# Row maxima taken with the additions in two dilated groups, and chunk-end keys made from chunk-middle keys, in a hybrid decoder layer

## The chip, the cores and the metric

The kernel runs on one core of a Trainium2 chip. The metric is the device time of one execution in microseconds, as the median of several runs. Five engines work side by side, each through its own queue in order: PE (TensorE, matrix products), DVE (VectorE), ACT (ScalarE), POOL (GpSimd) and SP (SyncE, which here only issues transfers). They wait for each other through semaphores.

## The reference, cut to what matters

One decoder layer on 512 tokens of 1024 features: a SwiGLU half-step, a token-mixing step, a second SwiGLU half-step. The token mixing has three branches; the change touches two of them.

The first is a gated linear recurrence in chunks of 64 tokens (4 heads, 128 key and 128 value dimensions):

```python
b = jnp.cumsum(jnp.log(f), axis=2)
ref = b[:, :, C // 2 - 1:C // 2]
scores = jnp.einsum('bnchk,bnshk->bnhcs', q * jnp.exp(b - ref), k * jnp.exp(ref - b))
...
b_last = b[:, :, -1:]
kv = jnp.einsum('bnshk,bnshv->nbhkv', k * jnp.exp(b_last - b), v)
```

The second is attention in three dilated groups (4 heads each): group 0 in blocks of 128 neighbours, group 1 with every fourth token, group 2 with every sixteenth. Each group adds an ALiBi bias and a mask to its scores, takes the row maximum, exponentials and their sum; the groups are then weighted against each other by maxima and sums:

```python
s = s - slopes[:, None, None] * (delta * dil).astype(jnp.float32)
s = jnp.where(valid[:, None], s, -jnp.inf)
m = jnp.max(s, axis=-1)
p = jnp.exp(s - m[..., None])
```

The third branch, attention of the tokens into 256 memory tokens, is not edited, but its work stands next to the edited work in the queues.

## The kernel before, in words

Weights and activations are split into a high part and a rest, and each product is made of three matmuls (lines 381 and 399 to 401). Pairs of weight columns are projected together in seven block products (`pair`, line 411); their operands are sums of weight quarters, made on DVE (tiles `sum`, `sh`, `st`) and split by ACT (line 173) and DVE (line 168) into tiles `w`. Line 168 is the helper `tt`, through which nearly every DVE addition, subtraction or multiplication of two tensors goes, so DVE rows are told apart by their tiles. The copy of line 438 takes the first of a pair's four results out of its PSUM bank (pool `ps`, 5 banks).

`mixing` (line 1107) runs the steps of `ORDER`: the two recurrence pairs (`hg0`, `hg1`), the preparation of the memory (`prep`, whose norm is in `normed`, lines 198 to 211: squares on ACT in line 186, a factor on DVE in line 192 and POOL in line 195, the scaling on DVE in line 204, transposes on PE in line 390), the dilated pairs (`dil0`, `dil1`, two heads each), the queries for the memory (`mq0`, `mq1`) and the three output branches. Elementwise work of a step is a generator that is continued when the projected PE time has advanced by the latencies in `LAT`; a scheduler then places the instructions of each engine in an order from its own estimates, so an edit in one place can move rows of its neighbours.

In `hgrn` (line 801), for each of two heads: `b` is the running sum of the logarithms; line 836 subtracts the chunk's middle, line 837 subtracts `b` from the chunk's last value, over 128x512; five exponentials follow on ACT (lines 841 to 845; line 843 is that of the chunk-end difference, line 845 makes the 128x8 decays); four multiplications on DVE make `qd`, `kd`, `kl` and `qe`. `hgrn_out` (line 858) multiplies `kd` by `qd` on PE, transposes `kl`, forms the states and the output. Its two small tiles `hss` and `hr` have four buffers.

In `dil_scores` (line 914), group 0 adds the bias and takes the maximum in one DVE instruction (line 928; in the trace CUSTOM_DVE_ANT_0, with a DVE_READ_ACCUMULATOR2_ANT that writes the maximum). Groups 1 and 2 put the scores of four 128x128 blocks into one PSUM bank (pool `px`, 3 banks, shared by all the elementwise steps), add the bias in two DVE additions of 128x256 (line 936), and for group 2 take the maxima of groups 1 and 2 together by two reductions over 128x512 (line 938). Line 943 scales the maximum into `nm`, and four exponentials with sums follow on ACT (line 946).

`mem_attention` (line 763) makes scores on PE (line 386), maxima on DVE (lines 774 and 775), exponentials on ACT (line 778, which also frees the `px` bank), and after a division (lines 779 and 782) transposes, copies (line 790) and a product with the values.

Of the kernel before, what the change touches and what calls it, by code (L numbers as in the profile page):

```python
# [8 lines left out]
F32 = mybir.dt.float32  # L9
F32R = mybir.dt.float32r  # L10
U32 = mybir.dt.uint32
AF = mybir.ActivationFunctionType
ALU = mybir.AluOpType
AX = mybir.AxisListType
# [3 lines left out]
P = 128  # L18
T = 512
NT = T // P  # L20
# [10 lines left out]
NCH = T // CHUNK  # L31
# [21 lines left out]
class Layer:  # L53
# [747 lines left out]
    def hgrn(self, hp, f, q, og, vh, out):  # L801

        nc = self.nc
        heads = [2 * hp, 2 * hp + 1]
        ch = lambda x: x.rearrange("p (n c) -> p n c", c=CHUNK)
        full = [P, NCH, CHUNK]
        step = LAT['hg']

        qs = [self.slot() for _ in heads]
        for i in range(2):  # L810
            nc.scalar.activation(f[i], f[i], AF.Sigmoid)
            nc.scalar.activation(qs[i], q[i], AF.Sigmoid)
        for i in range(2):
            nc.scalar.activation(og[i], og[i], AF.Sigmoid)
        k = []
        for i, hd in enumerate(heads):
            lb, omlb = self.lb[:, hd:hd + 1], self.omlb[:, hd:hd + 1]
            yield step
            nc.vector.tensor_scalar(out=f[i], in0=f[i], scalar1=omlb, scalar2=lb, op0=ALU.mult, op1=ALU.add)
            k.append(self.slot())  # L820
            nc.vector.tensor_scalar(out=k[i], in0=f[i], scalar1=-1.0, scalar2=1.0, op0=ALU.mult, op1=ALU.add)
            self.tt(q[i], q[i], qs[i], ALU.mult)
        for i in range(2):
            nc.scalar.activation(f[i], f[i], AF.Ln)
        b, kd, qd, qe, kl, dec = [], [], [], [], [], []
        for i in range(2):
            yield step
            b.append(self.slot())
            nc.vector.tensor_tensor_scan(out=b[i], data0=self.reset, data1=f[i], initial=0.0, op0=ALU.mult, op1=ALU.add)
        for i in range(2):  # L830
            yield step
            ref = ch(b[i])[:, :, CHUNK // 2 - 1:CHUNK // 2]
            last = ch(b[i])[:, :, CHUNK - 1:CHUNK]
            kd.append(self.slot())
            kl.append(self.slot())
            self.tt(ch(kd[i]), ch(b[i]), ref.broadcast_to(full), ALU.subtract)
            self.tt(ch(kl[i]), last.broadcast_to(full), ch(b[i]), ALU.subtract)
            qd.append(self.slot())
            qe.append(self.slot())
            dec.append(self.sm(NCH, "dec"))  # L840
            nc.scalar.activation(qd[i], kd[i], AF.Exp)
            nc.scalar.activation(kd[i], kd[i], AF.Exp, scale=-1.0)
            nc.scalar.activation(kl[i], kl[i], AF.Exp)
            nc.scalar.activation(qe[i], b[i], AF.Exp)
            nc.scalar.activation(dec[i], last.rearrange("p n o -> p (n o)"), AF.Exp)
        for i in range(2):
            yield step
            self.tt(qd[i], qd[i], q[i], ALU.mult)
            self.tt(kd[i], kd[i], k[i], ALU.mult)
            yield step  # L850
            self.tt(kl[i], kl[i], k[i], ALU.mult)
            self.tt(qe[i], qe[i], q[i], ALU.mult)
        yield LAT['hgx']
        for i, hd in enumerate(heads):
            yield from self.hgrn_out(hd, kd[i], qd[i], kl[i], qe[i], dec[i], og[i], vh)
            out[hd] = og[i]

    def hgrn_out(self, hd, kd, qd, kl, qe, dec, og, vh):
        nc = self.nc
# [17 lines left out]
        st = [self.slot((P, 4, P)) for _ in range(2)]  # L877
# [20 lines left out]
            self.mm(po[rs, n // 2, :], qe[:, n * CHUNK:(n + 1) * CHUNK], state[n - 1], False, True, skip_group_check=True)  # L898
        sq = self.slot((P, NT, P))
        nc.scalar.activation(sq, po, AF.Square)  # L900
        ss, r = self.sm(NT, "hss"), self.sm(NT, "hr")
        nc.vector.tensor_reduce(out=ss, in_=sq, axis=AX.X, op=ALU.add)
        nc.vector.tensor_scalar(out=ss, in0=ss, scalar1=1.0 / P, scalar2=EPS, op0=ALU.mult, op1=ALU.add)
        nc.gpsimd.tensor_tensor(out=r, in0=ss, in1=self.mhalf, op=ALU.pow)
# [9 lines left out]
    def dil_scores(self, nb, g, q, k, s, st, then=None):  # L914

        nc = self.nc
        yield LAT['dil0']  # L920
        if g == 0:
            for j in range(NT):
                lo = max(0, j - 1) * P
                n = (j + 1) * P - lo
                sp = self.paux((P, n))
                self.mm(sp, q[:, j * P:(j + 1) * P], k[:, lo:lo + n])
                out = s[j // 2][:, j % 2, :, :].rearrange("p a b -> p (a b)")[:, 2 * P - n:]
                nc.vector.tensor_tensor_reduce(out=out, in0=sp, in1=nb[:, 2 * P - n:2 * P], scale=1.0, scalar=-3.0e38,
                                               op0=ALU.add, op1=ALU.max, accum_out=st[:, j, 0:1])
        else:  # L930
            sp = self.paux((P, 4, P))
            for a in range(4):
                self.mm(sp[:, a, :], q[:, a, :], k[:, a, :])
            nb = nb[:, (g + 1) * P:(g + 2) * P].unsqueeze(1).broadcast_to([P, 2, P])
            for i in range(2):
                self.tt(s[i][:, :, g - 1, :], sp[:, 2 * i:2 * i + 2, :], nb, ALU.add)
                if g == 2:
                    nc.vector.tensor_reduce(out=st[:, 2 * i:2 * i + 2, 0:1], in_=s[i].rearrange("p a g b -> p a (g b)"), axis=AX.X, op=ALU.max)  # L938
        if then is None:
            return  # L940
        yield LAT['exp']
        nm = self.sm(4, "nm")
        nc.vector.tensor_scalar(out=nm, in0=st[:, :, 0], scalar1=-SCALE, scalar2=None, op0=ALU.mult)
        for i in range(4):
            b = self.dil_block(s, i, g == 0)
            nc.scalar.activation(b, b, AF.Exp, bias=nm[:, i:i + 1], scale=SCALE, accum_out=st[:, i, 1:2])
            if i == 1:
                yield LAT['exp']
        then()
# [393 lines left out]
```

## Time and profile before

| what | value |
|---|---|
| median of 3 runs | 1344.18 us (1342.6 to 1344.91) |
| profiled execution, its own time | 1344.03 us |
| its span, first to last instruction | 1342.3 us |
| mean granted TensorE clock in it | 0.998 |
| DVE busy | 1042.6 us (78%) in 1976 instructions |
| ACT busy | 755.4 us (56%) in 1557 instructions |
| POOL busy | 88.4 us (7%) |

The page gives busy time of each engine, the chain of work that ended last, and groups of instructions with the idle time before them and what ended it. The trace behind it gives every instruction with its start and length. An instruction's length is longer than its share of the engine, because the next one starts before it ends; the distance from start to start is the share. Matmul ends are modelled, so waits of PE are read from starts. The edited work lies between 425 and 760 us.

### The profile page before, as it was taken

What the parts mean: (1) busy time and instruction counts of PE and PEld (TensorE: products, weight loads), DVE (VectorE), ACT (ScalarE), POOL (GpSimd) and SP (SyncE); (2) the same over time, 40 slices, a digit from 0 to 9 for tenths busy, and PEclk for the clock granted to TensorE, in tenths of its full rate; (3) what the DMA queues carried; (4) which work ended last, traced back from release to release, by engine and by line L of the source; (5) the groups of instructions that cost most, each with busy time, mean ns of one, the idle gap of its engine ahead of it and who ended that gap; (6) DMA issues with size and microseconds to landing.
All of it is one profiled execution on the core that took longest, in us unless ns stands there. A gap on an engine that the chain in (4) does not pass through costs nothing.

```text
span 1342.3 us, 24319 instructions
## 1 busy us (share of the span) xinstructions
PE 1328.7 (99%) x9223; PEld 1234.9 (92%) x9223; DVE 1042.6 (78%) x1976; ACT 755.4 (56%) x1557; POOL 88.4 (7%) x117
## 2 busy tenths in 40 slices
PE   9999999999999999999999999999999999999997
PEld 7999999999898988899899999999899999999996
DVE  6987777688797976599868968898578877777765
ACT  7675545456467665355675755566366654455541
POOL 1011110110100000000000000000010111111101
PEclk9999999999999999999999999999999999999999
DMA  9587566565524335434223323324635666555513
GB/s 251 132 191 183 142 157 156 122 162 170 173 82 151 110 95 170 128 104 129 69 77 113 104 81 109 103 88 147 213 110 157 176 172 153 145 142 153 146 63 126
DMA packets 238607, 183.14 MB, mean 136 GB/s; under 512 B 11127, under 2 KB 200984, under 8 KB 238490
## 3 DMA queue, kind: packets, MB, share of 16 engines
q1 hardware_dynamic: 223702, 159.49, 39.5%
q0 software_dynamic: 10368, 18.88, 8.5%
q10 hardware_dynamic: 4420, 3.22, 0.8%
q8 instruction: 72, 1.18, 0.4%
q14 instruction: 45, 0.37, 0.1%
HBM read 153.21 MB, written 9.47 MB: 121 GB/s over the span
## 4 chain that ended last, share of the span: by engine, by line
PE 63%; DVE 2%; DMA 1%; ACT 1%; issue 0%; POOL 0%; DVEq 0%; POOLq 0%; ACTq 0%
PE ps L381 16%; PE ps L399 12%; PE ps L400 12%; PE ps L401 12%; PE px L381 7%; PE px L386 4%; PE px L390 1%; DVE s L168 1%; DVE w L168 1%; ACT s L186 0%; DMA sh<-in_w_in_dram 0%; DMA sum<-in_w_in_dram 0%; DVE s L266 0%; POOL r L195 0%; DVE st L938 0%
## 5 line engine op out<-in xcount | busy, mean ns | idle before, releaser
L173 ACT ACTIVATE w<-sum 128x512 fp32r<-128x512 f32 x288 | 180.4, 631 | 207.3 <-PE ps L400 180.4
L168 DVE TENSOR_TENSOR w<-sum,w 128x512 fp32r<-128x512 f32 x288 | 197.1, 688 | 79.4 <-ACT w L173 78.1
L400 PE MATMUL ps<-xlo,w 128*128 128x256 f32 x864 | 245.0, 284 | 0.0
L399 PE MATMUL ps<-xhi,w 128*128 128x256 f32 x864 | 244.9, 283 | 0.0
L401 PE MATMUL ps<-xhi,w 128*128 128x256 f32 x864 | 244.5, 283 | 0.0
L173 ACT ACTIVATE w<-st 128x512 fp32r<-128x512 f32 x240 | 150.2, 630 | 117.0 <-PE ps L400 87.3
L168 DVE TENSOR_TENSOR w<-st,w 128x512 fp32r<-128x512 f32 x248 | 168.8, 688 | 34.0 <-ACT w L173 32.1
L381 PE MATMUL px<-s,s 128*128 128x512 f32 x816 | 193.0, 390 | 0.4 <-DVE s L168 0.4
L168 DVE TENSOR_TENSOR s<-s,s 128x256 f32<-128x256 f32 (+3 forms) x316 | 176.8, 565 | 15.9 <-ACT s L173 2.9
L381 PEld LDWEIGHTS px<-s,s 128*128 128x128 f32 x816 | 150.6, 188 | 30.3 <-DVE s L168 0.8
L399 PEld LDWEIGHTS ps<-xhi,w 128*128 128x128 f32 x864 | 165.5, 192 | 2.3 <-ACT s L423 0.2
L400 PEld LDWEIGHTS ps<-xlo,w 128*128 128x128 f32 x864 | 165.5, 192 | 2.0
L401 PEld LDWEIGHTS ps<-xhi,w 128*128 128x128 f32 x864 | 165.5, 192 | 0.0
L168 DVE TENSOR_TENSOR sum<-sum,st 128x512 f32<-128x512 f32 x176 | 120.4, 687 | 5.1 <-DMA st<-in_w_in_dram 1.9
L168 DVE TENSOR_TENSOR s<-s,ps 128x256 f32<-128x256 f32 (+1 forms) x195 | 93.1, 478 | 27.7 <-PE ps L381 20.4
L399 PE MATMUL ps<-t3hi,w 128*128 128x256 f32 x288 | 82.8, 288 | 0.0
L399 PE MATMUL ps<-t1hi,w 128*128 128x256 f32 x288 | 82.2, 285 | 0.0
L399 PE MATMUL ps<-t4hi,w 128*128 128x256 f32 x288 | 82.2, 285 | 0.0
L400 PE MATMUL ps<-t4lo,w 128*128 128x256 f32 x288 | 81.9, 284 | 0.0
L400 PE MATMUL ps<-t3lo,w 128*128 128x256 f32 x288 | 81.8, 284 | 0.0
L401 PE MATMUL ps<-t1hi,w 128*128 128x256 f32 x288 | 81.5, 283 | 0.0
L400 PE MATMUL ps<-t2lo,w 128*128 128x256 f32 x288 | 81.5, 283 | 0.0
(195 smaller groups left out, 2971.4 us busy)
## 6 DMA issues: line engine op xcount, KB each, us to landing
st<-in_ffn_w_gu_dram SPq DMA_DIRECT2D x48, 512.0 KB, 5.0
st<-in_w_in_dram SPq DMA_DIRECT2D x48, 512.0 KB, 3.7
st<-in_ffn_w_down_dram SPq DMA_DIRECT2D x44, 512.0 KB, 4.6
sum<-in_ffn_w_gu_dram SPq DMA_DIRECT2D x80, 256.0 KB, 3.2
sh<-in_ffn_w_gu_dram SPq DMA_DIRECT2D x40, 256.0 KB, 3.2
sum<-st POOLq DMA_DIRECT2D x40, 256.0 KB, 3.4
sum<-sh POOLq DMA_DIRECT2D x32, 256.0 KB, 3.6
sum<-in_w_in_dram SPq DMA_DIRECT2D x32, 256.0 KB, 3.0
```

The source lines that it names most:

```text
L168: ins = self.nc.vector.tensor_tensor(out=out, in0=a, in1=b, op=op)
L173: self.pin(self.nc.scalar.activation(hi, src, AF.Copy))
L381: self.pin_pe(mm(out, lhsT=lhs[l], rhs=rhs[r], start=a, stop=b))
L386: self.nc.tensor.matmul(out, lhsT=lhsT, rhs=rhs, start=start, stop=stop, **k)
L390: self.pin_pe(self.nc.tensor.transpose(out, in_, self.ident))
L399: mm(out, lhsT=lh, rhs=rh, start=first and k == 0, stop=False, skip_group_check=True)
L400: mm(out, lhsT=lh, rhs=rl, start=False, stop=False, skip_group_check=True)
L401: mm(out, lhsT=ll, rhs=rh, start=False, stop=k == 3, skip_group_check=True)
```

## The change

For the recurrence, the difference to the chunk's end is no longer made per element. A tile `end` of 128x8 per head holds last minus middle for the eight chunks; its exponential is taken on ACT; and `kl` is the finished `kd` times `end`, broadcast over each chunk. `hss` and `hr` go from four buffers to two. For the dilated groups 1 and 2, addition and maximum come in one DVE instruction per 128x128 block, four per group and head, each with its accumulator read; group 1 writes its maxima to `st`, group 2 to a small tile from the pool of `nm`, and one 128x4 maximum joins them.

```diff
-        b, kd, qd, qe, kl, dec = [], [], [], [], [], []
+        b, kd, qd, qe, kl, dec, end = [], [], [], [], [], [], []
...
             self.tt(ch(kd[i]), ch(b[i]), ref.broadcast_to(full), ALU.subtract)
-            self.tt(ch(kl[i]), last.broadcast_to(full), ch(b[i]), ALU.subtract)
+            end.append(self.small.tile([P, NCH], F32, tag="end", bufs=2, name=f"end{self.uid()}"))
+            self.tt(end[i].unsqueeze(2), last, ref, ALU.subtract)
...
             nc.scalar.activation(kd[i], kd[i], AF.Exp, scale=-1.0)
-            nc.scalar.activation(kl[i], kl[i], AF.Exp)
+            nc.scalar.activation(end[i], end[i], AF.Exp)
...
             self.tt(kd[i], kd[i], k[i], ALU.mult)
             yield step
-            self.tt(kl[i], kl[i], k[i], ALU.mult)
+
+            self.tt(ch(kl[i]), ch(kd[i]), end[i].unsqueeze(2).broadcast_to(full), ALU.mult)
...
-        ss, r = self.sm(NT, "hss"), self.sm(NT, "hr")
+        ss, r = [self.small.tile([P, NT], F32, tag=n, bufs=2, name=f"{n}{self.uid()}") for n in ("hss", "hr")]
...
-            nb = nb[:, (g + 1) * P:(g + 2) * P].unsqueeze(1).broadcast_to([P, 2, P])
-            for i in range(2):
-                self.tt(s[i][:, :, g - 1, :], sp[:, 2 * i:2 * i + 2, :], nb, ALU.add)
-                if g == 2:
-                    nc.vector.tensor_reduce(out=st[:, 2 * i:2 * i + 2, 0:1], in_=s[i].rearrange("p a g b -> p a (g b)"), axis=AX.X, op=ALU.max)
+
+            mx = st[:, :, 0:1] if g == 1 else self.sm(4, "nm").unsqueeze(2)
+            for a in range(4):
+                nc.vector.tensor_tensor_reduce(out=s[a // 2][:, a % 2, g - 1, :], in0=sp[:, a, :], in1=nb[:, (g + 1) * P:(g + 2) * P],
+                                               scale=1.0, scalar=-3.0e38, op0=ALU.add, op1=ALU.max, accum_out=mx[:, a, :])
+            if g == 2:
+                self.tt(st[:, :, 0:1], st[:, :, 0:1], mx, ALU.max)
```

The change also moves rows. In the changed kernel the lines above shift by 2 to 4 (the exponential of `end` is line 844, the new instruction of the groups line 939, its `nm` line 947, the exponentials of the groups line 950, the scaling of the blocks line 992).

**ACT, between the exponentials of the first recurrence head and the squares of the memory's norm (`prep`).** Before:

```order
L841 ACTIVATE s_5398<-s_5394 128x512
L844 ACTIVATE s_5399<-s_5372 128x512
L842 ACTIVATE s_5394<-s_5394 128x512
L843 ACTIVATE s_5395<-s_5395 128x512
L186 ACTIVATE s_5410,ss_1109_5409<-s_5283 128x512
L186 ACTIVATE s_5413,ss_1111_5412<-s_5284 128x512
```

Now:

```order
L842 ACTIVATE s_5399<-s_5394 128x512
L844 ACTIVATE end_5397<-end_5397 128x8
L845 ACTIVATE s_5400<-s_5372 128x512
L843 ACTIVATE s_5394<-s_5394 128x512
L186 ACTIVATE s_5411,ss_1110_5410<-s_5283 128x512
L186 ACTIVATE s_5414,ss_1112_5413<-s_5284 128x512
```

Ahead of the squares stands one exponential of 128x512 less and one of 128x8 more. On PE the fourth group of four transposes of this norm comes five matmuls earlier than before.

**DVE, where the first dilated pair ends and the memory's maxima begin** (`s_..<-s_..,c_..` scales blocks of the dilated attention, `mmx` and `mnm` are the memory's maxima, `px` their banks). Before:

```order
L988 TENSOR_SCALAR s_6821<-s_6821,c_8077 128x256 x2
L988 TENSOR_SCALAR s_6822<-s_6822,c_8077 128x256
L774 TENSOR_REDUCE mmx_7926<-px_8000 128x2
L988 TENSOR_SCALAR s_6822<-s_6822,c_8077 128x256
L775 TENSOR_SCALAR mnm_7927<-mmx_7926 128x2
L774 TENSOR_REDUCE mmx_7926<-px_8007 128x2
```

Now:

```order
L992 TENSOR_SCALAR s_6825<-s_6825,c_8089 128x256 x2
L992 TENSOR_SCALAR s_6826<-s_6826,c_8089 128x256 x2
L168 TENSOR_TENSOR w_8417<-sum_8274,w_8416 128x512
L774 TENSOR_REDUCE mmx_7938<-px_8012 128x2
L774 TENSOR_REDUCE mmx_7938<-px_8019 128x2
L775 TENSOR_SCALAR mnm_7939<-mmx_7938 128x2
```

Between the last scaling and the first `mnm` there now stand a split of 128x512 and a second maximum. On PE the last score product of this head pair, which takes the bank that the first maximum and its exponentials free, stands four matmuls later than before.

**ACT, at group 2 of the first dilated pair's second head** (`s_7920<-ps_7769` is the copy out of the projection's bank). Before:

```order
L173 ACTIVATE w_8110<-sum_7963 128x512
L426 COPY s_7788<-ps_7831 128x256
L438 COPY s_7920<-ps_7769 128x256
L946 ACTIVATE s_6821,st_0_6810<-s_6821,nm_7867 128x256 x2
L946 ACTIVATE s_6822,st_0_6810<-s_6822,nm_7867 128x256 x2
L173 ACTIVATE w_8126<-sh_7938 128x512
```

Now:

```order
L426 COPY s_7798<-ps_7841 128x256
L173 ACTIVATE w_8122<-sum_7975 128x512
L173 ACTIVATE w_8138<-sh_7950 128x512
L950 ACTIVATE s_6825,st_0_6814<-s_6825,nm_7879 128x256 x2
L950 ACTIVATE s_6826,st_0_6814<-s_6826,nm_7879 128x256 x2
L438 COPY s_7932<-ps_7769 128x256
```

The copy now stands behind the four exponentials and a split. At three of the four places where group 2 ends, it is moved so. On SP one weight-quarter load (tile `sum`) moves behind the two bias loads of the second dilated pair; the orders of the other loads and of POOL stay.

## Rows read from the trace of the kernel before

**Rows 1.** Page, part 1: busy us, share of the span, instructions.

```profile
PE 1328.7 (99%) x9223; PEld 1234.9 (92%) x9223; DVE 1042.6 (78%) x1976; ACT 755.4 (56%) x1557; POOL 88.4 (7%) x117
```

**Rows 2.** Waits of PE and PEld, 400 to 860 us: total us, times, longest.

```profile
PE px L386 <- ACT s L778: 1.3, 1, 1.3
PE px L390 <- DVE s L204: 0.9, 1, 0.9
PE px L386 <- DVE st L928: 0.2, 1, 0.2
...
PEld px L386 <- DVE st L928: 1.1, 3, 0.5
```

**Rows 3.** Windows: us, busy by engine (PE, PEld, DVE, ACT, POOL), PEclk, DMA, GB/s.

```profile
640.00:660.00 20.00, 18.67 (x129) 16.47 (x129) 17.58 (x60) 16.42 (x48) 0.00 (x0) 1.00 0.21 57
```

**Rows 4.** Timeline, memory norm, 431 to 438 us: start, length, engine, instruction, [idle before].

```profile
431.88 0.62 ACT L843 ACTIVATE s<-s 128x512 f32<-128x512 f32 x1
432.40 0.62 ACT L186 ACTIVATE s<-s 128x512 f32<-128x512 f32 x1
...
433.75 0.21 DVE L192 TENSOR_SCALAR v<-ss,ss 128x1 f32<-128x1 f32 x1 [0.29 <-ACT s L186]
...
437.73 0.63 PE L390 MATMUL px<-ident,s 128*128 128x128 f32 x4 [0.91 <-DVE s L204]
```

**Rows 5.** Timeline of ACT at 628 us: a 128x8 exponential and its successor.

```profile
628.82 0.21 ACT L980 ACTIVATE wt<-wt 128x8 f32<-128x8 f32 x1
628.94 1.14 ACT L173 ACTIVATE w<-sum 128x512 fp32r<-128x512 f32 x2
```

**Rows 6.** Timeline of DVE: group 0 at 576 us, group 2 at 624 us.

```profile
575.87 0.28 DVE L928 CUSTOM_DVE_ANT_0 s<-px,s 128x128 f32<-128x128 f32 x1
576.08 0.08 DVE L928 DVE_READ_ACCUMULATOR2_ANT st<- 128x1 f32 x1
576.08 0.69 DVE L168 TENSOR_TENSOR sum<-sum,st 128x512 f32<-128x512 f32 x1
...
623.83 0.75 DVE L168 TENSOR_TENSOR s<-px,s 128x256 f32<-128x256 f32 x2
624.49 1.27 DVE L938 TENSOR_REDUCE st<-s 128x2 f32<-128x512 f32 x2
625.68 0.42 DVE L168 TENSOR_TENSOR s<-s,s 128x256 f32<-128x256 f32 x1
```

**Rows 7.** Timeline, memory scores, 645 to 655 us: DVE, ACT and PE.

```profile
645.18 0.69 DVE L774 TENSOR_REDUCE mmx<-px 128x2 f32<-128x512 f32 x1
646.04 0.16 DVE L775 TENSOR_SCALAR mnm<-mmx 128x2 f32<-128x2 f32 x1
...
646.29 0.47 ACT L778 ACTIVATE s<-px,mnm 128x256 f32<-128x256 f32 x1 [3.58 <-DVE mnm L775]
653.82 1.05 ACT L790 COPY s<-px 128x512 f32<-128x512 f32 x2
...
645.76 0.28 PE L401 MATMUL ps<-t3hi,w 128*128 128x256 f32 x1
647.37 1.13 PE L386 MATMUL px<-s,s 128*128 128x256 f32 x4 [1.33 <-ACT s L778]
654.59 1.88 PE L386 MATMUL px<-s,s 128*128 128x512 f32 x4
```

**Rows 8.** Timeline, group 2 of the second head, 636 to 640 us: ACT and PE.

```profile
635.93 0.37 ACT L438 COPY s<-ps 128x256 f32<-128x256 f32 x1 [0.61 <-PE ps L401]
637.60 0.51 ACT L946 ACTIVATE s<-s,nm 128x256 f32<-128x256 f32 x1 [1.30 <-DVE nm L943]
640.05 0.28 PE L399 MATMUL ps<-t2hi,w 128*128 128x256 f32 x1
```

**Rows 9.** Timeline of SP, the loads at 662 us.

```profile
661.90 0.37 SPq L155 DMA_DIRECT2D sum<-in_w_in_dram  x1
662.37 1.62 SPq L145 DMA_DIRECT2D s<-in_nbias_dram  x2
```

## The prediction, made before the changed kernel ran

> **What bounds the kernel now.** I read the page first: PE is busy for 1328.7 of the span's 1342.3 us, DVE for 1042.6, ACT for 755.4 [rows 1]. What a change on DVE or ACT is worth is therefore not its busy time but what it takes out of PE's waits. So the second view is the list of those waits between 400 and 860 us, where the edited work and its neighbours lie [rows 2]: the matmuls waited 1.3 us for an exponential of the memory attention (ACT L778), 0.9 us for the scaling of the memory's norm (DVE L204) and 0.2 us for a maximum of group 0 (DVE L928); the weight loads beside them waited 1.1 us for group 0 in three places. That is some 3.5 us in all. The third view, the windows, tells where DVE is the engine that the others wait for: from 640 to 660 us PE is busy for only 18.67 of 20 us, with DVE at 17.58 and ACT at 16.42 [rows 3]. The timelines of the two largest waits [rows 4, 7] then give what stands ahead of each.
>
> **The recurrence: what is removed.** Per head, one subtraction over 128x512 (a row of that form is 0.69 us on DVE [rows 6]) becomes one over 128x8; a small row of DVE is 0.16 us [rows 7], so about 0.53 us go, 2.1 us for four heads. One exponential over 128x512 becomes one over 128x8: from start to start the large one takes 0.52 us (431.88 to 432.40) [rows 4], the small one 0.12 us (628.82 to 628.94) [rows 5], so 0.40 us of ACT go per head, 1.6 us in all. The multiplication that makes `kl` stays, over the same 128x512; its broadcast operand I price like the subtraction before it, which broadcast too. None of this is PE work.
>
> Where it meets PE is one place. The third group of transposes of the memory's norm starts at 437.73, having waited 0.91 us for DVE L204 [rows 4]. Behind it stands a chain: L204 waits for POOL's factor, that for L192, and L192 began at 433.75 after an idle 0.29 us that ACT's squares (L186) ended. The exponential of line 843 stood directly ahead of these squares. With it gone and the 128x8 one in, the squares end 0.40 us earlier; DVE is no limit, since a subtraction and a multiplication (0.69 each) leave its queue ahead of L192 for two small rows (0.16 each), about 1.1 us. So PE's wait shrinks from 0.91 to about 0.5: **-0.4 us**. Bounds: 0 if POOL or DVE takes it back, -0.9 if the wait goes. I take the row of the idle, which names ACT. The fourth group of transposes now comes five matmuls earlier and needs a `px` bank that DVE and ACT empty; they have to have read the first group's bank, which they do 0 to 0.3 us too late by adding up rows of 0.42 and 0.69 behind L204. I take 0.1.
>
> The new dependence, `kl` on `kd` and `end`, delays `kl` behind one multiplication (0.69); PE transposes `kl` only behind the projection that separates the norm's third and fourth transposes and behind the products of `kd` and `qd`, and that hides it; without this cover it would cost 0.7 per head. Two buffers less for `hss` and `hr` cost nothing: a third head takes them only when the first head has long been normalised.
>
> **The groups: what is exchanged.** Group 1 loses two additions over 128x256, group 2 the same and two reductions. From 623.83 to 625.68 these four take 1.85 us [rows 6]; two additions alone, 0.66 (623.83 to 624.49). What comes in is shown by group 0: the combined instruction over 128x128 starts at 575.87 and its successors at 576.08, the read of the accumulator and the next addition at the same time [rows 6]. Four of these are 0.84 us. So group 1 costs +0.18 per head and group 2 0.84 + 0.16 (the 128x4 maximum) - 1.85 = -0.85. Over four heads: DVE saves 2.7 us. The scores' bank is held 0.18 us longer; the next product that takes a `px` bank is a projection away, so I price that at 0.
>
> The Trainium skill speaks against this exchange (VectorE: DVE Perf Modes, Rules for kernel authors): do not fuse chained DVE instructions for speed, count instructions instead, because the pipe is emptied behind each. The change adds 43 DVE rows. The trace does not bear the rule out for this instruction: the successors start 0.21 us after it, before its own 0.28 us are over. By the rule, the saving would be lost in the added rows and the time would be that of the second rival below.
>
> Where this meets PE is the wait before 647.37. PE had stopped after the matmul of 645.76 and waited 1.33 us for a `px` bank; ACT L778 freed it, starting at 646.29, because DVE's `mnm` came at 646.04, behind a full queue of DVE [rows 7]. Two groups 2 lie ahead: 1.7 us saved. But the new order puts a split (0.69) and a second maximum (0.69) ahead of the first `mnm`, about 1.3 us from start to start, which leaves `mnm` 0.4 us earlier (bounds: 0 and 1.7). On PE four matmuls, some 0.5 us, now stand ahead of the waiting product, so its wait falls from 1.33 to about 0.5. That is not all kept: behind it ACT works through eight exponentials, eight scalings and two copies to 654.87 (653.82 plus 1.05), and PE's product of 654.59 needs those copies [rows 7]. ACT's chain moves by the 0.4 us of `mnm` and no more. So PE is 0.4 earlier at the end of this stretch: **-0.4 us** (bounds 0 and -1.3).
>
> Elsewhere: the second dilated pair saves 1.3 us of DVE beside a PE without a wait, worth nothing now. The waits for group 0 (0.2 and 1.1) lie behind splits and loads that the change leaves, so they stay. On ACT the copy L438 moves behind four exponentials at three places. At the tightest, the old exponentials started at 637.60 and take four times 0.51; with the copy's 0.37 it would end at 640.0, and the product that takes this bank two allocations later starts at 640.05 [rows 8]. `nm` comes earlier there, by 0.85 and more, so it costs nothing; if it came later, every 0.1 us would count. On SP the quarter load at 661.90 goes behind two bias loads whose issue takes 1.62 us [rows 9]; its quarter belongs to a pair whose other quarters come four loads later on SP. POOL's order stays.
>
> **The sum.** -0.4 + 0.1 - 0.4 = -0.7 us against the profiled execution's 1344.03, that is 1343.3. The median of the runs, 1344.18, is 0.15 above that execution; I forecast **1343.3 us**, with -0.3 to -1.5 as the reach of this case. About 0.2% (2.7 us) is what a measurement of this kernel can tell from no change, so this case is "same".
>
> **The rivals.**
> 1. All waits go: if DVE alone holds PE in this part and the savings carry through, up to the 3.5 us of [rows 2] go: 1340.5. For it: each wait has DVE in its chain. Against it: the order puts new rows ahead of `mnm`, and the waits for group 0 lie where nothing is saved.
> 2. The new instruction costs its full rows, 0.28 + 0.08, so that four take 1.44 us. Then group 2 saves 0.25 per head instead of 0.85, `mnm` comes 0.8 us later than before through the added rows, and the four matmuls ahead of the wait cover 0.5 of that: +0.3, less 0.4 of the norm: 1344.0. For it speaks nothing in [rows 6], where the read overlaps.
> 3. Slower: the moved copy L438 decides. If a group of four takes twice its full rows, 2.9 us, `nm` comes 1.2 us later than before; the copy then holds its PSUM bank past 640.05, and PE's second product of the next pair waits for it at three places. The tightest has 0.05 us of slack, so PE loses about 1.2 us at each: +3.6, less 0.4: 1347.2. It decides from the point where `nm` is later than before by more than the slack. Against it: 0.21 us per instruction.
> 4. The change does not do what it says: the scheduler's other moved rows (DVE has about a hundred places) cancel the two gains, or add one small wait: 1343.5 to 1345.
>
> **How the numbers follow.** Forecast 0.55, rival 1 0.10, rival 2 0.15, rival 3 0.05, rival 4 0.15. The single runs before spread from 1342.6 to 1344.91, so a median can lie half a microsecond off by itself. The range has to take in the forecast's reach, rivals 2 and 4, and lies between rival 1 and rival 3, leaving most of each out: 1341.0 to 1345.5. Faster than 1341.5 is rival 1 and a little of the forecast: 0.12. Slower than 1346.9 is rival 3 and a little of rival 4: 0.06. The rest, 0.82, is the same.
>
> **What would show it.** Right: line 843's successor (128x8) near 0.2 us, the squares 0.4 us earlier, PE's wait for L204 near 0.5; combined rows 0.21 us apart in groups 1 and 2; the wait for L778 near 0.5 with the following product some 0.4 to 0.8 us earlier; DVE's busy time lower by 3 to 5 us with PE's span nearly as it was. Wrong: combined rows further apart than 0.3 us, a wait of PE `ps` for ACT L438 (then rival 3), or waits of PE in places that have none now.

## The result, and the profile after

The change made the kernel slower by a little. Over 17 runs of each the median went from 1344.45 us (1342.6 to 1345.68) to **1346.94 us** (1344.53 to 1349.25); the ratio is **1.0019**, with a 95% interval of 1.0012 to 1.0025, about 2.5 us. The runs after also lie further apart, 4.7 us against 3.1. The profiled execution took 1345.61 us (span 1343.8), at a granted clock of 0.998 as before.

The work did shrink. Part 1 of the page, to be held against [rows 1], shows DVE 4.6 us and ACT 2.7 us lighter in 44 more DVE instructions:

```profile
PE 1329.3 (99%) x9223; PEld 1235.2 (92%) x9223; DVE 1038.0 (77%) x2020; ACT 752.7 (56%) x1557; POOL 88.5 (7%) x117
```

The waits of PE and PEld between 400 and 860 us, to be held against [rows 2], show that the waits stayed and that a new one joined them, for the copy of line 408 (a pair's first product leaves its PSUM bank there):

```profile
PE px L386 <- ACT s L778: 1.0, 1, 1.0
PE px L390 <- DVE s L204: 0.9, 1, 0.9
PE ps L399 <- ACT s L408: 0.6, 1, 0.6
...
PEld px L386 <- DVE st L930: 0.9, 3, 0.3
PEld ps L399 <- ACT s L408: 0.8, 1, 0.8
```

The new wait stands in the projection of the second recurrence pair (`hg1`). The timeline of the changed kernel gives its chain, engine by engine: PE, ACT, DVE, and the two loads on SP.

```profile
463.74 0.28 PE L401 MATMUL ps<-t3hi,w 128*128 128x256 f32 x1
464.58 0.39 PE L399 MATMUL ps<-xhi,w 128*128 128x256 f32 x1 [0.56 <-ACT s L408]
...
462.34 1.28 ACT L811 ACT_TABLE_LOAD   x1 [3.04 <-DVE s L168]
463.64 0.63 ACT L811 ACTIVATE s<-s 128x512 f32<-128x512 f32 x1
464.17 0.35 ACT L408 COPY s<-ps 128x256 f32<-128x256 f32 x1
...
450.05 0.67 DVE L168 TENSOR_TENSOR w<-st,w 128x512 fp32r<-128x512 f32 x1
456.39 0.69 DVE L168 TENSOR_TENSOR sum<-sum,sh 128x512 f32<-128x512 f32 x1 [1.12 <-issue]
461.85 0.41 DVE L168 TENSOR_TENSOR s<-s,ps 128x256 f32<-128x256 f32 x1
...
450.75 0.38 SPq L155 DMA_DIRECT2D st<-in_w_in_dram  x1
452.56 0.37 SPq L155 DMA_DIRECT2D sh<-in_w_in_dram  x1
```

The same split, addition and loads in the kernel before:

```profile
446.16 0.69 DVE L168 TENSOR_TENSOR w<-st,w 128x512 fp32r<-128x512 f32 x1
454.77 0.69 DVE L168 TENSOR_TENSOR sum<-sum,sh 128x512 f32<-128x512 f32 x1
...
446.88 0.38 SPq L155 DMA_DIRECT2D st<-in_w_in_dram  x1
451.77 0.37 SPq L155 DMA_DIRECT2D sh<-in_w_in_dram  x1
```

Read from the bottom. In the new order a split that frees a weight buffer (`w<-st`) starts at 450.05; before, it started at 446.16. SP issues the next `st` load (512 KB) only at 450.75 instead of 446.88, and the `sh` quarter (256 KB) follows 1.8 us behind it, not 4.9. DVE comes to the addition that needs this quarter and stands there for 1.12 us. The profile names nothing for it ("issue"), but the traffic of these two loads has only just ended: the DMA view of the stretch from 450 to 458 us, in slices of 0.2 us, falls to nothing at 455.8, 0.6 us ahead of the addition. That it is this load that DVE waits for is so far inferred; the kernels with three buffers below bear it out.

```profile
GB/s 0 0 0 0 82 0 0 0 31 133 133 195 174 236 369 389 430 287 223 110 138 218 253 259 151 100 82 38 26 0 0 0 0 0 0 0 0 0 0 0
```

Behind the standing addition wait the states of the recurrence and the pair's own sums; the sum at 461.85 ends at 462.26, the table of the sigmoid of line 811 is loaded at 462.34, and only behind that sigmoid does ACT copy the bank that PE wants. From 463.74 to 464.58 PE issues nothing, where such matmuls otherwise follow each other in 0.12 us: 0.7 us.

How far each place contributes, and what is chance, shows when the same PE instruction is compared across profiles. The table gives, for stretches of PE's order, by how much a profile fell behind (+) or gained (-) on the kernel before; each number is the change of (start here minus start in the first profile of before), in us. The experiments below are already in it.

| profile | opening, to 11 | first FFN, to 412 | norm, to 440 | to 462 | to 472 | to 639 | memory scores, to 672 | to the end |
|---|---|---|---|---|---|---|---|---|
| before, second profile | +0.97 | +0.17 | -0.02 | +0.02 | 0 | +0.01 | -0.39 | +0.31 |
| the change | +1.05 | -0.01 | -0.43 | +0.45 | **+0.82** | 0 | -0.07 | -0.27 |
| the change, second profile | -0.42 | -0.74 | -0.41 | +0.27 | **+0.82** | +0.01 | **+2.75** | +1.21 |
| groups alone | -0.08 | -1.04 | -0.03 | +0.04 | 0 | +0.01 | +0.53 | +0.21 |
| recurrence alone | +0.36 | -1.12 | -0.42 | +0.60 | **+0.83** | +0.01 | -0.89 | +0.52 |
| change, addition held | +0.88 | +0.20 | -0.44 | +0.28 | 0 | +0.01 | -0.68 | +0.25 |
| change, first `mnm` first | +1.06 | -0.94 | -0.44 | +0.46 | **+0.81** | +0.01 | **+2.32** | +0.25 |
| change, three `sh` buffers | -0.21 | -0.25 | -0.45 | +0.30 | 0 | -0.29 | -1.19 | +0.05 |
| before, three `sh` buffers | +0.65 | -0.70 | -0.01 | +0.01 | 0 | -0.27 | -1.40 | +0.71 |

The first two columns are chance: no edit reaches there but the third buffer, and they scatter by about a microsecond with and without the change; in the opening it is the load of the second half of the first x block, whose square starts between 6.3 and 8 us. So one profile tells a difference of 2.5 us only by its places, not by its span. The border between the last two columns is uncertain by 0.3 us in the row "first `mnm` first", where PE's order differs around it.

### The profile page after: what moved, and what is told of

The parts are those of the page before. It is cut to its first block, busy times and chain, and to the rows that moved or that the text cites. A ratio compares the mean times of both kernels' runs of the same rounds, so it can differ in the third digit from the quotient of the medians.

```text
span 1343.8 us, 24364 instructions
## 1 busy us (share of the span) xinstructions
PE 1329.3 (99%) x9223; PEld 1235.2 (92%) x9223; DVE 1038.0 (77%) x2020; ACT 752.7 (56%) x1557; POOL 88.5 (7%) x117
## 4 chain that ended last, share of the span: by engine, by line
PE 86%; DVE 7%; ACT 3%; DMA 2%; issue 2%; POOL 1%; DVEq 0%; SPq 0%; POOLq 0%; ACTq 0%
PE ps L399 17%; PE ps L400 17%; PE ps L401 17%; PE ps L381 17%; PE px L381 14%; PE px L386 4%; DVE w L168 2%; DVE s L168 2%; PE px L390 2%; DMA s<-in_x_dram 1%; DVE sum L168 1%; ACT s L186 1%; POOL r L195 1%; DVE s L266 1%; DMA s<-in_ffn_post_w_dram 1%
## 5 line engine op out<-in xcount | busy, mean ns | idle before, releaser
L401 PE MATMUL ps<-t2hi,w 128*128 128x256 f32 x288 | 81.6, 283 | 0.0
```

The source lines that it names most:

```text
L401: mm(out, lhsT=ll, rhs=rh, start=False, stop=k == 3, skip_group_check=True)
```

## The experiments

**First, each part alone, and both kernels again.** The groups alone are the edit of `dil_scores`; the recurrence alone is all the rest of the diff. Theory A puts the loss on the recurrence edit and its late load, theory B on the groups edit, theory C on the opening.

> The groups edit alone; the recurrence is that of the kernel before, and so is DVE's order of rows there. Theory A (the recurrence edit costs: its moved DVE rows release a stage buffer later, a load lands later, DVE stands at the addition that needs it, and PE waits some 0.8 us for ACT L408 near 463 us): the ratio is 0.999 to 1.000, no PE wait for L408, and what is left of the opening's 1 us is chance. Theory B (the groups edit costs): the ratio is about 1.002, as with the whole change. Theory C (the opening is later with every changed program, by 1 us): the second half of the first x block is squared at 7.9 us instead of 6.8 us here too, and the ratio is about 1.0005.

> The recurrence edit alone (with the two buffers for the head's sums); the groups are those of the kernel before. Its DVE order around the first recurrence pair is that of the whole change. Theory A: ratio 1.001 to 1.003, and PE waits again 0.5 to 0.8 us (and PEld as much) for ACT L408 near 463 us. Theory B: ratio 0.999 to 1.000. Theory C: the first x block's second half is squared at 7.9 us here too.

> The whole change once more, for a second profile. Theory A: the wait for L408 near 463 us is there again (0.5 us or more), ratio 1.001 to 1.003. Theory C: the square of the second half of the first x block starts at 7.9 us again; if the late load was chance it starts nearer to 6.8 us, as before.

> The kernel before once more, for a second profile of its opening. If the first x loads scatter by themselves, the square of the second half of the first x block does not start at 6.8 us again but anywhere between 6.5 and 8 us; theory C has 6.8 us again. No wait for L408 near 461 us by theory A.

Groups alone: ratio 1.0008 [0.9999, 1.0016]. Recurrence alone: 1.0006 [0.9997, 1.0015]. The change again: 1.0019 [1.0010, 1.0028]. Before again: 0.9996 [0.9986, 1.0006]. Neither part alone can be told from no change. Theory B, that the groups carry the loss, falls: it wanted about 1.002. Theory A wanted 0.999 to 1.000 for the groups and 1.001 to 1.003 for the recurrence; both medians miss that, and the intervals just reach it. The two parts, 1.1 and 0.8 us, together are 1.9 of the 2.5 us. The opening (theory C) is chance: the square in question started at 7.89 us in the second profile of before, at 6.31 in the second of the change. The new wait, though, is there in each profile that has the recurrence edit in its plain order (0.81 to 0.83 us in the table) and in none without it.

The second profile of the change shows a place that the first had hidden: PE waited 2.4 us for L778 in the memory scores, where before it waited 1.3 and in the first profile of the change 1.0.

```profile
PE px L386 <- ACT s L778: 2.4, 1, 2.4
...
PE ps L399 <- ACT s L408: 0.6, 1, 0.6
```

The waiting product starts 1.32 to 1.34 us behind the first `mnm` in all nine profiles that have this wait, so the wait follows how late `mnm` is against PE. Part of that is read on DVE, between 597 and 648 us of the second profile, in the rows where DVE waits for the `sh` quarter of a dilated pair and the first `mnm`:

```profile
608.64 0.69 DVE L168 TENSOR_TENSOR sum<-sum,sh 128x512 f32<-128x512 f32 x1 [1.34 <-DMA sh<-in_w_in_dram]
620.16 0.69 DVE L168 TENSOR_TENSOR sum<-sum,sh 128x512 f32<-128x512 f32 x1 [1.32 <-DMA sh<-in_w_in_dram]
632.82 0.69 DVE L168 TENSOR_TENSOR sum<-sum,sh 128x512 f32<-128x512 f32 x1 [0.43 <-DMA sh<-in_w_in_dram]
...
647.12 0.17 DVE L775 TENSOR_SCALAR mnm<-mmx 128x2 f32<-128x2 f32 x1
```

Before, with `mnm` at 646.04 [rows 7]:

```profile
608.35 0.69 DVE L168 TENSOR_TENSOR sum<-sum,sh 128x512 f32<-128x512 f32 x1 [0.97 <-DMA sh<-in_w_in_dram]
619.03 0.69 DVE L168 TENSOR_TENSOR sum<-sum,sh 128x512 f32<-128x512 f32 x1 [0.86 <-DMA sh<-in_w_in_dram]
632.08 0.69 DVE L168 TENSOR_TENSOR sum<-sum,sh 128x512 f32<-128x512 f32 x1 [0.73 <-DMA sh<-in_w_in_dram]
```

From the first of these additions to `mnm` it took 37.7 us before and 38.5 here, though DVE has less to do in the whole run. The waits for `sh` already existed before (2.8 us between 575 and 648 us); in this profile they are 3.5, in the first profile of the change 2.0.

The longer wait is only half of the 2.8 us that lie between the two profiles of the change. The other half is TensorE's clock. The windows give its granted share (the third value from the end) behind the wait, first for the second profile of the change, then for the first; the rows behind them are PE's timeline in the second.

```profile
648.80:652.20 3.40, 3.40 (x15) 3.12 (x14) 2.31 (x8) 3.40 (x14) 0.00 (x0) 0.51 0.00 0
...
648.80:652.20 3.40, 2.77 (x20) 2.66 (x21) 3.18 (x13) 3.40 (x15) 0.00 (x0) 1.00 0.00 0
...
648.45 1.72 PE L386 MATMUL px<-s,s 128*128 128x256 f32 x4 [2.40 <-ACT s L778]
...
650.39 0.41 PE L399 MATMUL ps<-t3hi,w 128*128 128x256 f32 x1
650.61 0.41 PE L400 MATMUL ps<-t3lo,w 128*128 128x256 f32 x1
```

The clock fell from 1.00 (2.4 GHz) to 0.50 (1.2 GHz) at 648.9 us, right behind the wait of 2.4 us, and was back at 652.3. In between, matmuls that otherwise follow each other in 0.12 us came 0.21 apart. Against the first profile the wait makes PE 1.4 us later and the slow stretch 1.5. Only one other profile of the thirteen has such a fall before the run's last microseconds: the kernel "first `mnm` first", with a wait of 1.9 us here and 0.50 from 649.2 to 652.6. In the others, with 1.6 us and less, the clock stayed at 1.00. The mean clocks of the single runs point the same way: 0.997, a value that none of the 99 such runs of the kernel before shows, stands at 4 of 17 and 4 of 11 runs of the change, at 3 of 11 with the groups alone and at 4 of 9 with the first `mnm` first, and at none of 11 with the recurrence alone (one run each of two kernels further down has it too). In each of the four sets that have it the runs at 0.997 took 1.0 to 2.0 us longer in the mean than the others.

**Then, four runs to tell the two places apart.** In the first, `HELD` counts the column pairs, and 25 is the second of `hg1`; in the second, only the order of the maxima is set, and the scheduler moved other rows behind it; the last two differ from the change and from before by one buffer (with 36 slots alone the order of every engine stays as it was; that kernel was not run). From here on theory C stands for something else: late loads of `sh` in the dilated pairs.

```diff
+                if j == 1:
+                    low1.append(self.last_low)
...
-            with self.tc.issue_after(self.opened[0]):
+            with self.tc.issue_after(self.opened[0]), self.tc.issue_after(low1[0]) if held and low1 else nullcontext():
                 return sums_of(n)
```

```diff
-            nc.vector.tensor_reduce(out=mx[:, two], in_=s, axis=AX.X, op=ALU.max)
-            nc.vector.tensor_scalar(out=nm[:, two], in0=mx[:, two], scalar1=-SCALE, scalar2=None, op0=ALU.mult)
+            with self.tc.issue_after(first.ins) if i else nullcontext():
+                nc.vector.tensor_reduce(out=mx[:, two], in_=s, axis=AX.X, op=ALU.max)
+            first = nc.vector.tensor_scalar(out=nm[:, two], in0=mx[:, two], scalar1=-SCALE, scalar2=None, op0=ALU.mult)
```

```diff
-NSLOT = 37
+NSLOT = 36
...
-        a22 = self.stage.tile([P, 4, P], F32, tag="st2", bufs=2, name=f"sh{self.uid()}")
+        a22 = self.stage.tile([P, 4, P], F32, tag="st2", bufs=3, name=f"sh{self.uid()}")
```

> The whole change, with one row of DVE put back: the addition of the `sh` quarter in the second column pair of the second recurrence projection is issued behind the split of that pair's `st` block, and so no longer stands at the head of DVE's queue while its load is in flight. PE's, SP's and POOL's orders are those of the whole change. Theory A (that waiting addition costs the 0.7 us near 463 us): PE's and PEld's waits for ACT L408 (0.6 and 0.8 us) go or fall under 0.2, and the ratio falls from 1.0019 to about 1.0013. Rival (ACT's own order makes L408 late): the wait stays at 0.6 and the ratio at 1.002.

> The whole change, with the second maximum of each memory head's scores issued behind the first `mnm`, as it was in the kernel before. Theory B (the groups edit moves a maximum and a split ahead of the first `mnm`, which eats what the combined rows save): from the last addition of an `sh` quarter before it to the first `mnm` it takes 13.6 to 13.8 us, not 14.3, PE's wait for ACT L778 is 0.5 us shorter than at the same PE lead, and the ratio is about 1.0015. Rival (it was late loads alone that made DVE late): the ratio stays at 1.002, since `mnm` is late by what DVE waits for `sh` (1.3 us twice).

> The whole change with three buffers for the `sh` quarter instead of two, so that its load goes out one column pair earlier, paid for with one of the 37 slots. Theory C (what the combined rows save in DVE is given back as waits for `sh` loads that are issued close behind other loads): DVE's waits for `sh` between 575 and 648 us (2.0 to 3.5 us) fall under 0.7, PE's wait for ACT L778 falls under 0.5, and the kernel stands 0.5 to 1.5 us under its counterpart of the kernel before (next run). Rival (DVE's own rows bound it): the waits for `sh` go but `mnm` comes no earlier, and the change still costs 2 us against its counterpart.

> The kernel before with the same three `sh` buffers and 36 slots, as the counterpart. Theory C: its waits for `sh` (2.8 us between 575 and 648 us) go as well, and it is 0 to 1 us faster than the kernel before; the change is then worth minus 0.5 to minus 1.5 us. Rival: same time as the kernel before, and the changed kernel 2 us above it. If the missing slot costs something, it shows in both.

*Addition held:* ratio 1.0004 [0.9995, 1.0012], and the wait for L408 near 463 us is gone. (This profile has another of 0.6 us, for the copy of its line 428, at 407 us; it lies ahead of the held row, in the stretch that is chance.) What was held is the second pair's addition; the one that had been standing is the third pair's, and it came along, from ahead of the states to behind them, and some other rows of DVE and ACT up to 478 us moved too. The loads went out at the same times as in the change (450.80 and 452.55), so it was not the load that changed but what stood in the queue when it was late. In this kernel, whose lines are 5 and more further down (L816 is L811, L413 is L408), the addition is DVE's row at 462.87, without idle time, and ACT starts a microsecond earlier:

```profile
462.87 0.69 DVE L169 TENSOR_TENSOR sum<-sum,sh 128x512 f32<-128x512 f32 x1
...
461.25 1.28 ACT L816 ACT_TABLE_LOAD   x1 [2.41 <-DVE s L169]
462.54 0.63 ACT L816 ACTIVATE s<-s 128x512 f32<-128x512 f32 x1
463.08 0.35 ACT L413 COPY s<-ps 128x256 f32<-128x256 f32 x1
```

Theory A holds for this place. The gain on the whole, about 2 us, is more than the 0.8 us of the place; the memory scores lost nothing in this profile either (-0.68), with 1.3 us of waits for `sh` between 575 and 648 us instead of 2.0 and 3.5 in the two profiles of the change, and none of this kernel's 11 runs shows the clock of 0.997. Whether the one follows from the other these runs don't tell.

*First `mnm` first:* 1.0023 [1.0013, 1.0033], which cannot tell theory B's 1.0015 from the rival's 1.002. From the last `sh` addition to the first `mnm` it took 13.85 us, 0.45 less than in the change, nearly as expected: so much the order of the maxima is worth. But DVE had waited 1.46 and 1.28 us for `sh` on the way there, PE still waited 1.9 us for L778, and the clock fell behind that wait.

*Three buffers:* the changed kernel took 1342.26 us, 0.9992 [0.9983, 1.0001], its counterpart of before 1342.55 us, 0.9991 [0.9982, 1.0000]. With the `sh` loads one column pair ahead, neither kernel has a wait of DVE for `sh` between 575 and 648 us, and the only PE wait that the profile lists between 400 and 860 us, in either, is that for the norm; the changed kernel's:

```profile
PE px L390 <- DVE s L204: 0.9, 1, 0.9
```

Between the two the change is worth -0.3 us, which is no difference. So theory C had the remedy right and the gain wrong (-0.5 to -1.5 expected): with the loads a pair ahead the 2.5 us are gone, and the change costs nothing and brings nothing. From the addition at 606 us to `mnm` DVE still takes 0.5 us longer with the change (37.9 us against 37.4), but it gets there early enough that PE no longer waits. Theory C's mechanism, that saved rows come back as waits for `sh`, does not hold in the mean: between 575 and 648 us DVE waited 2.0, 3.5, 2.7, 1.3 and 2.7 us for `sh` in the five profiles with the new groups and two buffers, and 2.8, 2.3, 1.3 and 2.9 in the four with the old. Both kernels lie a good microsecond under the kernel before, with intervals that reach 1.000. The third buffer serves every column pair of the kernel, so rows move in the half-steps too; the table puts most of the gain into the stretch of the memory scores.

**Last, the order alone, one more gain, and a repeat.** The first of these changes the kernel before, with `BACK` the first pair of `hg1`; the second is the change with three buffers and one exponential moved; the third is the change with three buffers again.

```diff
+        self.ahead = total
...
+            behind = back and j == 2
+            if behind:
+                self.ahead("s1")
+                added = self.last_low
-            with self.tc.issue_after(self.opened[0]), self.tc.issue_after(self.opened[1]):
+            with self.tc.issue_after(self.opened[0]), self.tc.issue_after(self.opened[1]), self.tc.issue_after(added) if behind else nullcontext():
                 return operand(j)
```

```diff
-            nc.scalar.activation(qe[i], b[i], AF.Exp)
...
         for i in range(2):
             yield step
+            nc.scalar.activation(qe[i], b[i], AF.Exp)
             self.tt(qd[i], qd[i], q[i], ALU.mult)
```

> The kernel before, arithmetic untouched, with only the order that the change brought: the last split of the `st` block of the first column pair in the second recurrence projection is issued behind the next pair's additions, so that the next load into this buffer goes out later and the addition of `sh` stands at the head of DVE's queue. SP's order stays. Theory A (this order alone makes the wait): PE waits 0.5 to 0.8 us for ACT L408 near 463 us as in the changed kernel, and the ratio is 1.0005 to 1.0015. Rival (the wait needs the new arithmetic of the keys, `kl` behind `kd`): no wait for L408, ratio 1.000.

> The changed kernel with three `sh` buffers, and the exponential that decays the queries (`qe`) issued one step later, behind the norm's squares on ACT. Theory (the norm's place follows ACT, as the step of the prediction had it): the squares end another 0.5 us earlier and PE's third group of norm transposes comes 0.4 to 0.5 us earlier; with no other waits left the kernel stands 0.3 to 0.5 us under the one with three buffers alone: ratio 0.9985 to 0.999. Rival (POOL's and DVE's rows of the norm take it back, or `qe` comes late for the outputs): ratio 0.999 to 1.0.

> The changed kernel with three `sh` buffers once more, for a second profile and more times. Theory C: ratio 0.9985 to 0.9995, no wait of DVE for `sh` between 575 and 648 us and no wait of PE for L778 or L408 whatever the opening did. Rival (the gain was chance): ratio 1.000 or more, with such waits again.

*The order alone* did not make the wait: 0.9999 [0.9990, 1.0008]. The split moved from 446.16 to 448.42 and the two loads to 449.13 and 451.42, 2.3 us apart; the addition stood for 0.26 us only, and PE did not wait:

```profile
449.13 0.38 SPq L156 DMA_DIRECT2D st<-in_w_in_dram  x1
451.42 0.37 SPq L156 DMA_DIRECT2D sh<-in_w_in_dram  x1
...
454.39 0.69 DVE L169 TENSOR_TENSOR sum<-sum,sh 128x512 f32<-128x512 f32 x1 [0.26 <-DVE w L169]
```

In the changed kernel the rows of the new `kl` and of the norm's last third come on top, and its loads follow each other in 1.8 us. So theory A, that this order alone makes the wait, is not borne out: the split moved by 2.3 us here and by 3.9 in the change. Which of the added rows make up the rest was not taken apart.

*The late exponential:* 1342.14 us, 0.9986 [0.9977, 0.9994]: faster than the kernel before and than the change. Between 412 and 440 us PE gained 0.95 us against 0.45 with three buffers alone, as expected, but by 462 us it had given back 0.63 against 0.30, with a new wait of 0.4 us at the norm's fourth transposes. *Three buffers again:* 1342.27 us, 0.9983 [0.9974, 0.9992], with the same waits as the first time although its opening was 1.1 us later. The late exponential adds nothing to it that these runs could tell; the gain of the changed kernel over the kernel before, 1.1 and 2.3 us in the two measurements, is that of the third `sh` buffer.

## Why the prediction was wrong, step by step

The forecast was 1343.3 us (1341.0 to 1345.5), 82% for no difference that a measurement can tell. The runs gave 1346.94, 1.4 us beyond the range, and a ratio at the bound of 0.2%: a loss of 2.5 us where a gain of 0.7 was forecast.

- **The prices held.** In group 2 four combined rows came 0.21 us apart, 0.84 in all, as taken from [rows 6], and the small maximum behind them starts 0.12 us after the last read:

```profile
626.44 0.28 DVE L939 CUSTOM_DVE_ANT_0 s<-px,s 128x128 f32<-128x128 f32 x1
626.65 0.08 DVE L939 DVE_READ_ACCUMULATOR2_ANT nm<- 128x1 f32 x1
...
627.28 0.08 DVE L939 DVE_READ_ACCUMULATOR2_ANT nm<- 128x1 f32 x1
627.40 0.17 DVE L168 TENSOR_TENSOR st<-st,nm 128x4 f32<-128x4 f32 x1
```

  DVE's saving was put at 4.8 us and is 4.6; the added rows are 44, not 43. The Trainium skill's rule not to fuse chained DVE instructions but to count them (VectorE: DVE Perf Modes, Rules for kernel authors) would, as the prediction read it, have eaten this saving in the added rows; the trace does not bear it out for this instruction, whose two rows, 0.28 and 0.08 long, take 0.21 us together.
- **The norm's place: right.** The sum had -0.4 us. Between 412 and 440 us PE gains 0.41 to 0.45 us in seven profiles with the recurrence edit, and 0.03 at the most in four without. In the timeline of the changed kernel the squares start 0.6 us later than in [rows 4], in a PE that is 1.04 us late from its opening at 412 us:

```profile
433.01 0.62 ACT L186 ACTIVATE s<-s 128x512 f32<-128x512 f32 x1
437.45 1.41 DVE L204 SCALAR_TENSOR_TENSOR s<-s,r,s 128x512 f32<-128x512 f32 x2 [0.66 <-POOL r L195]
438.34 0.63 PE L390 MATMUL px<-ident,s 128*128 128x128 f32 x4 [0.88 <-DVE s L204]
```

  That the wait itself would shrink from 0.91 to 0.5 was wrong: it reads 0.88, because PE came to it earlier too: the second group of transposes no longer stood 0.2 us behind the first.
- **The fourth transposes: too small.** Taken at 0.1, at most 0.3; at 444 us PE loses 0.27 to 0.30 us in the same seven profiles. In three of them it loses another 0.2 to 0.3 at 461 us, just ahead of the new wait, so that between 440 and 462 us it is 0.38 in the mean. So norm and transposes together gain nothing.
- **The failed step of the recurrence: "Where it meets PE is one place."** It meets PE at a second one, 25 us later: +0.82 us in four profiles of four with the plain order. The step followed the elementwise rows on DVE and ACT, and not the splits that stand between them on DVE, which release the weight buffers and so set when SP loads. The prediction had asked for this in its last sentence ("waits of PE in places that have none now"), but had put no price on it beyond rival 4's "one small wait".
- **The failed step of the groups: the memory scores at -0.4 us.** `mnm` was to come earlier by 1.7 us of saved rows less 1.3 for rows moved ahead of it. That sum lacks the prediction's own +0.18 for each of the two groups 1 that lie ahead as well; with them nothing is left. The runs show as much: from the addition at 608 us to `mnm`, without idle time, DVE's rows take 35.9 to 36.1 us in four profiles with the old groups and 36.0 in four with the new and the plain order of `mnm`. With idle time it took 37.0 to 37.7 us (37.4 in the mean) and 37.7 to 38.5 (38.0): `mnm` came 0.7 us later, not 0.4 earlier. This difference is idle time, which the step did not price: 1.4 us in the mean before, 2.0 with the new groups. Of the 0.6 more, 0.4 is a wait for ACT's split (line 173) at 629 to 632 us that the old order does not have, 0.1 the `sh` quarters, the rest gaps under 0.15 us. The bounds, 0 and -1.3, had excluded a loss without naming a reason.
- **A cost that stands in no step: the clock.** In two profiles PE's wait for L778 reached 1.9 and 2.4 us, and 3.4 us at half the granted clock followed. In the second profile of the change that made 1.5 us of the +2.75.
- **What was rightly put at nothing:** the copy L438 (no wait for it, so rival 3 did not come), the loads swapped on SP, the second dilated pair, and `kl` behind `kd`. The waits for group 0 stayed about as they were, as said.

Of the rivals, the fourth had the mechanism, moved rows that cancel the gains and add waits; its size, up to 1345, was too small by two. By their spans the two profiles of the change lie 1.5 and 3.5 us above the first of the kernel before, and the median's 2.5 between them: 0.8 us at the new wait in both, nothing and 2.75 at the memory scores, and the rest in the stretches that are chance and behind the scores.

The same kernel loses nothing at the memory scores in one profile and 2.75 us in another because `mnm` came 1.4 us later there, against PE, and the clock then fell. What stays open is what makes `mnm` so late in one execution and not in the other. DVE's longer waits for `sh` (3.5 us against 2.0) are as large as the difference. The time from issue to addition of the first late `sh` load was 3.2 to 4.3 us in five profiles with the new groups, whose `sum` and `sh` loads go out 1.1 us apart, and 2.9 to 3.25 us in four with the old, 2.1 us apart. That closer loads land later after their issue fits; what decides between 3.2 and 4.3 at the same spacing was not found. Nor was the 1.21 us taken apart that the second profile loses behind the scores.

## What to carry to other kernels

On an engine that works its queue in order, a row that frees a load's buffer and a row that needs a load are worth more than their length: when an edit moves rows, look for both among the rows that it moves, and follow the load through SP to the row that will stand at the head of the queue. Idle time inside a stretch has to be priced with its rows: saved rows need not be saved time there. Here a spare buffer that lets the load go out one step earlier brought what the lighter arithmetic did not, so it is worth trying first. Where PE's wait grows, read the granted clock behind it: here half of the loss of the worse profile was not the wait but what followed it. And where single runs scatter by as much as the effect, compare the start of the same instruction in several profiles place by place, rather than the spans.

## What the runs showed of the hardware that was not expected

A wait of PE can cost more than its length. Behind waits of 1.9 and 2.4 us at the memory scores the granted clock was 0.50 for 3.4 us, and matmuls came 0.21 us apart instead of 0.12; in the worse of the two this cost 1.5 us. Behind 1.6 us and less at the same place the clock stayed at 1.00 in these profiles.

The same program with the same loads got its second half of the first x block between 6.3 and 8 us after the start, and PE's work behind it lies between 0.42 us earlier and 1.06 later than in the first profile of before. Not all of this lasts: of the 1.06 us, 0.12 were left at 412 us.

And of two loads on one queue the second mostly took longer from its issue, the closer it was issued behind the first. The `sh` quarter at 603 to 607 us landed 3.1 to 4.2 us after its issue in the five profiles where it went out 1.1 us behind another 256 KB load, and 2.8 to 3.1 in four where it was 2.1 us. In the recurrence it took 3.8 us to the addition that needed it when 1.8 us behind a 512 KB block (452.56 to 456.39), and 3.0 at the most when 2.3 us behind it (451.42 to 454.39).
